# A recurrent layer's gates packed in three tiles of 128 rows, with the input split ahead of the gather

## The chip, the cores and the metric

One core of a Trainium2 chip runs the whole kernel. The metric is the device time of one execution in microseconds, the median of three runs. TensorE (PE) multiplies matrices, VectorE (DVE), ScalarE (ACT) and GpSimd (POOL) work on elements, and SyncE (SP) sends nearly all transfers; each engine takes its own instructions in order and waits for the others by semaphores.

## The reference, cut to what matters

The kernel computes two layers of a diffusion block on 512 latent and 256 context tokens. The change lies in the mixer of the second layer, a bidirectional gated linear recurrence with 16 heads of 88 channels (`D_RNN` = 1408):

```python
def rglru_coeffs(xb, w_a, b_a, w_x, b_x, lam):
    xh = xb.reshape(b, L, RG_HEADS, RG_DH)
    r = jax.nn.sigmoid(jnp.einsum('blhd,hde->blhe', xh, w_a).reshape(b, L, D_RNN) + b_a)
    gi = jax.nn.sigmoid(jnp.einsum('blhd,hde->blhe', xh, w_x).reshape(b, L, D_RNN) + b_x)
    log_a = (-RG_C * r) * jax.nn.softplus(-lam)
    a = jnp.exp(log_a)
    bx = jnp.sqrt(-jnp.expm1(2.0 * log_a)) * (gi * xb)
    return a, bx

# in bidir_rglru_mixer, for the latent tokens
z = h_lat @ w_in
gate = jax.nn.gelu(z[..., :D_RNN])
xl = depthwise_conv(z[..., D_RNN:], conv_w, conv_b, left=2)
af, bf = rglru_coeffs(xl, wa[0], ba[0], wx[0], bx[0], lam[0])
ab, bb = rglru_coeffs(xl, wa[1], ba[1], wx[1], bx[1], lam[1])
hf = linear_scan(af, bf, hf_c[:, -1], False)
hb = linear_scan(ab, bb, hb_c[:, 0], True)
y_lat = (gate * (hf + hb)) @ w_out
```

Each head thus has four gates: two (`wa`, `wx`) in each of two directions.

## The kernel before, in words

Channels lie on the 128 partitions, tokens along the free dimension, 768 of them (256 context, then 512 latent). Products in fp32 are made of three passes over two halves of each operand: a high half, which ACT or DVE casts to fp32r, and a low half, the difference. `mm3` (L260) sends the three passes, `split` (L256) makes the halves with `act.copy` and `dve.tensor_sub`, and `conv_w` with `halve` (L235, L247) does it for weights.

The recurrent mixer goes over 11 chunks of 128 channels, while the heads have 88 channels, so the two cut the 1408 channels differently; `rg_pieces` (L68) lists the 26 overlaps. For each chunk j:

- `xl_units(j)` (L1579) computes the input projection, 24 matmuls over each of two token ranges, and `xl_evac` (L1563) adds the convolution into a tile `xl` and sends the pieces of its rows by SP into one tile `hx` of 88 rows for each head (L1577).
- `head_units(h)` (L1635) splits `hx` into `xh` and `xlo`, and for each direction multiplies by the weights of two gates, 88 output rows each. ACT's `Tanh` (L1654) moves each gate from PSUM into a tile `tg`, two gates to a tile; the pieces go back by SP into tiles `th` that follow the chunks (L1660), one for each chunk and direction, four buffers in all.
- `rg_chunk(j)` (L1663) computes decay and input from `th` and `xl` (L1677 to L1692), scans (L1695 to L1699), multiplies with the gate and splits the result into `yh`, `yl`, written in place of `th` first (L1703 to L1707).
- `pg_units` (L1591) computes the product for the gate, and `w_out` (L1712) in three calls, after chunks 4, 7 and 10, the output product of three chunks with its addition to `x` in `residual` (L1081). The last two chunks' output product follows the stage.

`mix` (L1717) interleaves the heads of the next chunk with these products, so many units of filling for each unit of a head. The program's order is then a matter of a scheduler: the framework places the instructions of all engines by its own timeline, and each engine's order is fixed when the kernel is built. PSUM has two buffers of two banks (`mm`) for the heads and four of one bank (`sm`) for all else.

Of the kernel before, what the change touches and what calls it, by code (L numbers as in the profile page):

```python
# [9 lines left out]
F32 = mybir.dt.float32  # L10
F32R = mybir.dt.float32r
# [6 lines left out]
P = 128  # L18
# [29 lines left out]

PCOLS = {}
_n = 0  # L50
for _name, _w in (("b_ada0", 48), ("b_ada1", 48), ("mix_g0", 8), ("mix_g1", 8), ("ffn_g0", 8), ("ffn_g1", 8),
                  ("fin_g", 8), ("rcw", 44), ("rcb", 11), ("lam", 22),
                  ("c", 16), ("hcw", 36), ("hcb", 12), ("skip", 8), ("ln_g", 4)):
    PCOLS[_name] = (_n, _w)
    _n += _w
NPC = _n

NPL = PCOLS["c"][0]

PARTS = [[(i, min(i + 4, NPAIR)) for i in range(0, NPAIR, 4)], [(0, 20), (20, 22)]]  # L60

# [75 lines left out]
def layout(i):  # L137
    a = {}
    g = {k: np.asarray(v) for k, v in i.items()}
    xt = np.concatenate([g["ctx"][0], g["x"][0]], 0).T  # L140
    a["xs"] = np.ascontiguousarray(xt.reshape(KD, P, T))
    vec = lambda v: v.reshape(-1, P)
    rows = {
        "b_ada0": vec(g["b_ada"][0]), "b_ada1": vec(g["b_ada"][1]),
        "mix_g0": vec(g["norm_mix_g"][0]), "mix_g1": vec(g["norm_mix_g"][1]),
        "ffn_g0": vec(g["norm_ffn_g"][0]), "ffn_g1": vec(g["norm_ffn_g"][1]),
        "fin_g": vec(g["final_norm_g"]), "hcw": vec(g["hy_conv_w"][0]), "hcb": vec(g["hy_conv_b"][0]),
        "skip": vec(g["hy_skip"][0]), "ln_g": vec(g["sgu_ln_g"][0]), "rcw": vec(g["rg_conv_w"][0]),
        "rcb": vec(g["rg_conv_b"][0]),
        "lam": vec(g["rg_lam"][0]), "c": np.concatenate([vec(g["c"][0]), vec(g["c_ctx"])], 0),  # L150
    }
    a["prm"] = np.ascontiguousarray(np.concatenate([rows[k] for k in PCOLS], 0).T)
    a["w_ada"] = np.ascontiguousarray(g["w_ada"])
    a["wie"] = wtiles(g["w_in_even"][0])
    a["woe"] = wtiles(g["w_out_even"][0])
    a["wio"] = wtiles(g["w_in_odd"][0])
    a["woo"] = wtiles(g["w_out_odd"][0])
    for l in range(2):
        a[f"wfi{l}"] = wtiles(g["w_ffn_in"][l])
        a[f"wfo{l}"] = np.ascontiguousarray(wtiles(g["w_ffn_out"][l])[:, :, [k for p in PARTS[l] for k in paired(*p)]])  # L160
    rg = np.stack([g["rg_wa"][0], g["rg_wx"][0]], 1).transpose(3, 2, 0, 1, 4)
    a["rgw"] = np.ascontiguousarray(rg.reshape(RDH, NH // 2, 8 * RDH))
    hb = np.stack([g["rg_ba"][0], g["rg_bx"][0]]).reshape(64, RDH)
    a["hb"] = np.ascontiguousarray(hb.T)
    a["sw"] = np.ascontiguousarray(g["sgu_w"][0].transpose(2, 0, 1))
    a["sb"] = np.ascontiguousarray(g["sgu_b"][0].reshape(1, 512))
    a["f3w"] = np.ascontiguousarray(np.concatenate([g["hy_f3_w"][0], g["hy_f3_b"][0][None]], 0))
    c = constants()
    mlp = np.zeros((64, T + 131), np.float32)
    mlp[:33, 0:T] = c.pop("emb")  # L170
    mlp[:33, T:T + 64] = g["hy_f1_w"][0]
    mlp[:, T + 64:T + 128] = g["hy_f2_w"][0]
    mlp[:, T + 128:] = np.stack([g["hy_f1_b"][0], g["hy_f2_b"][0], g["hy_sin_freq"][0]], 1)
    a["mlp"] = mlp
    a.update(c)
    return a
# [3 lines left out]
def program(tc, A, out):  # L180
# [906 lines left out]
    def out_units(src, ks, xhi, xlo, off, mod_g, blks, nr=None, early=0, most=2):  # L1087

        n = len(ks)
        grp = min(most, 1024 // (n * P))  # L1090
        held, group = {}, []

        def weights(m):
            if W["rg"]:
                W["eng"] = dve, pool
            if grp == 1:
                return split_w(src(m), n * P)
            i = m % grp
            if i == 0:
                g = min(grp, KD - m)  # L1100
                with tc.high_priority(offset=W["pre"]):
                    raw = load_w(None, 0)
                    nc.sync.dma_start(raw[:, :g * n * P].rearrange("p (m c) -> p m c", m=g),
                                      src(slice(m, m + g)).rearrange("m p k c -> p m (k c)"))
                    group[:] = conv_w(raw, g * n * P)
            return [t[:, i * n * P:(i + 1) * n * P] for t in group]

        plan = [(m, b) for m in range(KD) for b in range(2)]
        h = max(KD - len(W["slots"]) * grp, 0)
        if nr:  # L1110
            plan = [(m, b) for m in range(h) for b in range(2)] + [(m, b) for b in range(2) for m in range(h, KD)]
        def unit(m, b, pa, part=slice(0, None)):
            t0, t1 = blks[b]
            wh, wl = held[m]
            for i, k in list(enumerate(ks))[part]:
                c = slice(k * P, (k + 1) * P)
                for pi, (w, x) in enumerate(((wh, xhi), (wh, xlo), (wl, xhi))):
                    pe.matmul(pa, w[:, c], x[k][:, t0 - off:t1 - off], start=(i == 0 and pi == 0),  # L1118
                              stop=(i == n - 1 and pi == 2))

        begun = {}
        if early:
            for m, b in plan[:4]:
                if b == 0:
                    held[m] = weights(m)
                begun[m, b] = smt()[:, 0:blks[b][1] - blks[b][0]]
                unit(m, b, begun[m, b], slice(0, early))
        for m, b in plan:
            t0, t1 = blks[b]
            if (m, b) in begun:  # L1130
                pa = begun[m, b]
                unit(m, b, pa, slice(early, None))
            else:
                if b == 0:
                    held[m] = weights(m)
                pa = smt()[:, 0:t1 - t0]
                unit(m, b, pa)
            residual(m, mod_g, pa, blks[b])
            if nr:
                nr.sumsq(m, xt[m], b, m > 4)  # L1140
                if b == 1 and m == (KD - 4 if grp > 1 and blks is SEGC else KD - 2 if grp > 1 else h):
                    nr.stats(0)
                if b == 1 and m == (KD - 1 if grp > 1 else h + 2):
                    nr.bc(0)
            yield
# [360 lines left out]
    sp = [spp.tile([P, 22], F32, name=f"sp{i}") for i in range(5)]  # L1506
    cq = c2.tile([P, 22], F32, name="cq")
    cq2 = c2.tile([P, 22], F32, name="cq2")
    hba = c2.tile([RDH, 64], F32, name="hba")
    nc.sync.dma_start(hba, A["hb"])  # L1510
    zz, nn, rr, ee, ss = sp
    dve.tensor_scalar_mul(zz, lam, -1.0)
# [50 lines left out]
    def xl_evac(j, ms):  # L1563
# [3 lines left out]
        for m, (c0, c1) in zip(ms, SEGC):  # L1567
            for kk, sh in ((0, -2), (1, -1), (3, 1)):
# [2 lines left out]
                dve.scalar_tensor_tensor(x[:, a:b], m[:, a + sh - c0:b + sh - c0], w, x[:, a:b],  # L1571
                                         op0=ALU.mult, op1=ALU.add)
        XL[j] = x
        for _, h, c0, h0, n in rg_pieces(j=j):
            if h not in HX:
                HX[h] = rg.tile([RDH, T], F32, tag="hx", bufs=2, name=nm("hx"))
            nc.sync.dma_start(HX[h][h0:h0 + n, :], x[c0:c0 + n, :])  # L1577

    def xl_units(j):  # L1579
        W["eng"] = act, dve  # L1580
# [54 lines left out]
    def head_units(h):  # L1635

        if h % 2 == 0:
            W["eng"] = act, dve
            HW[0] = split_w(A["rgw"][:, h // 2], 8 * RDH, rows=RDH)
        wh, wl = HW[0]  # L1640
        x = HX.pop(h)
        xh = wx.tile([P, 1024], F32R, tag="whi", bufs=1, name=nm("xh"))[0:RDH, 0:T]
        xl = wx.tile([P, 1024], F32R, tag="wlo", bufs=1, name=nm("xlo"))[0:RDH, 0:T]
        split(xh, xl, x)
        for d in range(2):
            t = rg.tile([RDH, 2, T], F32, tag="tg", bufs=2, name=nm("tg"))
            for mi in range(2):
                m = mmt()
                c = (h % 2 * 4 + d * 2 + mi) * RDH
                mm3([m[0:RDH, 0, 0:384], m[0:RDH, 1, 0:384]],  # L1650
                    [(wh[0:RDH, c:c + RDH], wl[0:RDH, c:c + RDH],
                      [xh[:, c0:c1] for c0, c1 in HALF], [xl[:, c0:c1] for c0, c1 in HALF])])
                b = 32 * mi + 16 * d + h
                act.activation(h3(t[:, mi, :]), m[0:RDH, :, 0:384], AF.Tanh, bias=hba[:, b:b + 1], scale=0.5)  # L1654
                if mi == 0:
                    yield
            for j, _, c0, h0, n in rg_pieces(h=h):
                if (j, d) not in TH:
                    TH[j, d] = rg.tile([P, 2, T], F32, tag="th", bufs=4, name=nm("th"))
                nc.sync.dma_start(TH[j, d][c0:c0 + n], t[h0:h0 + n])  # L1660
            yield

    def rg_chunk(j):  # L1663
# [46 lines left out]
    yh, yl = [], []  # L1710

    def w_out(k0, k1, nr=None):  # L1712
        return out_units(lambda m: A["woo"][m, :, k0:k1, :], range(k1 - k0), yh[k0:k1], yl[k0:k1], LC, g4, BLK1, nr)

    W["rg"] = True

    def mix(hs, fill, nf):  # L1717

        hu = [u for h in hs for u in [h] * 4]
        done = 0  # L1720
        gens = {h: head_units(h) for h in hs}
        for i, h in enumerate(hu):
# [20 lines left out]
    for j in range(NR):  # L1743
# [9 lines left out]
            n += 8  # L1753
        if j in (4, 7, 10):
            gens.append(w_out(j - 4, j - 1))
            n += 16
        if j == 4:
            dve.tensor_scalar_mul(g4, mod[1][1][:, :, 0:8], 0.25)
        gens.append(itertools.islice(last_mods, 1 if j > 4 else 2))
# [59 lines left out]
```

## Time and profile before

| | |
|---|---|
| median of three runs | 1833.41 us (1829.68 to 1834.64) |
| profiled execution, its own time | 1836.92 us |
| its span | 1835.1 us |
| PE / DVE / ACT / POOL busy in the span | 1689.9 / 1210.3 / 771.7 / 607.4 us |
| mean granted clock of PE, share of full | 0.955 |

The span runs from the first to the last instruction; the execution's own time is longer by what lies around it. A busy time is the sum over an engine's instructions. Matmuls are pipelined, so the distance between two starts says more of PE's pace than the duration of one, which holds a fill and a drain beside its columns.

### The profile page before, as it was taken

The numbers are of one execution on the slowest core, as the hardware profiler recorded it, in microseconds if no ns is written. First come the engines' busy times: TensorE is split into PE (matmuls) and PEld (weight loads), VectorE is DVE, ScalarE is ACT, GpSimd is POOL, SyncE is SP. The second block draws the span as 40 slices with busy tenths as digits, with TensorE's granted clock in tenths as the row PEclk, the third lists the DMA queues.
The fourth block names the chain that finished last, engine by engine and source line by source line (L and its number), as shares of the span: only waits on it lengthen the run. The fifth ranks groups of instructions, "written<-read, shape, count | busy, mean of one in ns | idle before, by whom it ended". The sixth has DMA issues, their size and how long they took to land. (4 is left out here: it accounts for less than half of the span.)

```text
span 1835.1 us, 23819 instructions
## 1 busy us (share of the span) xinstructions
PE 1689.9 (92%) x8968; PEld 1433.9 (78%) x8968; DVE 1210.3 (66%) x1883; ACT 771.7 (42%) x1224; POOL 607.4 (33%) x518
## 2 busy tenths in 40 slices
PE   5999999889889999999999898879996799999996
PEld 2576887679878989999999676667776778888885
DVE  7875766684887668777776848768889733333225
ACT  3643332222454555544454437655654432222212
POOL 4333132442466455655554213324343200000002
PEclk8999999899999999999999898889997899999998
DMA  8746232633115312121222145646553132222321
GB/s 289 233 146 235 87 113 72 244 113 127 58 39 179 116 58 81 58 81 58 81 69 69 58 134 168 191 125 177 157 170 108 48 126 92 92 92 83 89 81 46
DMA packets 78397, 213.00 MB, mean 116 GB/s; under 512 B 7610, under 2 KB 33354, under 8 KB 74186
## 3 DMA queue, kind: packets, MB, share of 16 engines
q1 hardware_dynamic: 75913, 204.67, 35.6%
q0 software_dynamic: 1792, 6.29, 0.9%
q8 instruction: 70, 1.15, 0.3%
q10 hardware_dynamic: 576, 0.52, 0.1%
q14 instruction: 46, 0.37, 0.1%
HBM read 178.30 MB, written 11.53 MB: 103 GB/s over the span
## 5 line engine op out<-in xcount | busy, mean ns | idle before, releaser
L250 DVE TENSOR_TENSOR wlo<-raw,whi 128x512 fp32r<-128x512 f32 (+2 forms) x300 | 307.4, 1039 | 311.0 <-ACT whi L249 305.0
L249 ACT CAST whi<-raw 128x512 fp32r<-128x512 f32 (+2 forms) x308 | 244.0, 810 | 421.3 <-PE mm L265 180.7
L397 POOL TENSOR_TENSOR ssum<-ssum,sq 128x256 f32<-128x256 f32 (+2 forms) x37 | 37.2, 1010 | 451.1 <-ACT sq L395 426.8
L250 POOL TENSOR_TENSOR wlo<-raw,whi 128x1024 fp32r<-128x1024 f32 (+1 forms) x31 | 75.0, 2421 | 143.7 <-DVE whi L249 73.4
L1118 PE MATMUL sm<-yh,whi 128*128 128x256 f32 (+1 forms) x304 | 98.4, 329 | 23.3 <-DVE x L1081 12.7
L1118 PE MATMUL sm<-yl,whi 128*128 128x256 f32 (+1 forms) x304 | 97.0, 319 | 0.0
L1118 PE MATMUL sm<-yh,wlo 128*128 128x256 f32 (+1 forms) x304 | 96.4, 318 | 0.0
L288 PE MATMUL sm<-hh,whi 128*128 128x512 f32 (+1 forms) x248 | 92.1, 372 | 1.2 <-DVE whi L249 0.7
L288 PE MATMUL sm<-hl,whi 128*128 128x512 f32 (+1 forms) x248 | 91.0, 367 | 0.0
L288 PE MATMUL sm<-hh,wlo 128*128 128x512 f32 (+1 forms) x248 | 90.4, 368 | 0.1
L1118 PEld LDWEIGHTS sm<-yh,whi 128*128 128x128 f32 x304 | 61.3, 203 | 29.8 <-DVE x L1081 15.0
L339 PE MATMUL sm<-ada,sct 128*32 128x512 f32 x384 | 74.5, 642 | 4.4 <-DMA ada<-in_w_ada_dram 2.8
L1654 ACT ACTIVATE tg<-mm,hba 88x768 f32<-88x768 f32 x64 | 55.8, 892 | 41.7 <-issue 22.8
L265 PE MATMUL mm<-hl,whi 128*128 128x512 f32 (+1 forms) x256 | 69.8, 347 | 0.0
L265 PE MATMUL mm<-hh,wlo 128*128 128x512 f32 (+1 forms) x256 | 69.3, 348 | 0.0
L265 PE MATMUL mm<-hh,whi 128*128 128x512 f32 (+1 forms) x256 | 68.5, 347 | 0.0
L1118 PEld LDWEIGHTS sm<-yl,whi 128*128 128x128 f32 x304 | 62.1, 204 | 0.0
L1118 PEld LDWEIGHTS sm<-yh,wlo 128*128 128x128 f32 x304 | 61.5, 203 | 0.0
L1332 POOL TENSOR_TENSOR u<-u,u 128x384 f32<-128x384 f32 x40 | 47.8, 1195 | 40.1 <-ACT u L1331 39.8
L288 PEld LDWEIGHTS sm<-hh,whi 128*128 128x128 f32 x248 | 48.6, 196 | 15.0 <-ACT whi L249 2.5
L1081 DVE SCALAR_TENSOR_TENSOR x<-sm,mod,x 128x128 f32<-128x128 f32 (+3 forms) x68 | 33.9, 501 | 35.2 <-PE sm L1494 18.1
L288 PEld LDWEIGHTS sm<-hh,wlo 128*128 128x128 f32 x248 | 48.3, 196 | 8.9 <-DVE wlo L250 0.9
(942 smaller groups left out, 5273.4 us busy)
## 6 DMA issues: line engine op xcount, KB each, us to landing
raw<-in_wfi_dram SPq DMA_DIRECT2D x88, 512.0 KB
ada<-in_w_ada_dram SPq DMA_DIRECT2D x32, 1024.0 KB
raw<-in_wfo_dram SPq DMA_DIRECT2D x38, 512.0 KB
ada<-in_w_ada_dram SPq DMA_DIRECT2D x24, 512.0 KB
raw<-in_wio_dram SPq DMA_DIRECT2D x22, 512.0 KB
raw<-in_wie_dram SPq DMA_DIRECT2D x20, 512.0 KB
th<-tg SPq DMA_DIRECT2D x12, 528.0 KB
kk<-kdx SPq DMA_DIRECT2D x16, 384.0 KB
```

The lines of the kernel that those rows point to most:

```text
L249: (h_.tensor_copy if h_ is not act else act.copy)(hi, src)
L250: l_.tensor_sub(lo, src, f(hi))
L265: pe.matmul(o, w, xx, start=(k == 0 and pi == 0), stop=(k == n - 1 and pi == 2))
L288: pe.matmul(self.outs[b], w[:, k * P:(k + 1) * P], x, start=(n == 0 and pi == 0), stop=(n == self.nk - 1 and pi == 2))
L339: pe.matmul(self.ps[32 * q:32 * q + 32, :], sct[:, 2 * k:2 * k + 32], self.w[k, q], start=(k == 0), stop=(k == KD - 1))
L397: (dve if late else pool).tensor_add(self.s[b], self.s[b], q)
L1081: dve.scalar_tensor_tensor(x, pa[:, s0 - t0:s1 - t0], mod_g[:, v, m:m + 1], x, op0=ALU.mult, op1=ALU.add)
L1118: pe.matmul(pa, w[:, c], x[k][:, t0 - off:t1 - off], start=(i == 0 and pi == 0), stop=(i == n - 1 and pi == 2))
L1332: pool.tensor_add(v, v, u)
L1654: act.activation(h3(t[:, mi, :]), m[0:RDH, :, 0:384], AF.Tanh, bias=hba[:, b:b + 1], scale=0.5)
```

## The change

Three parts, all in the recurrent mixer, and one of memory. (1) A head's four gates, 352 output rows, are cut into three tiles of 128, 128 and 96 rows instead of four of 88; a tile's rows belong to one, two or three gates, so the way back into `th` has more pieces, of 8 to 88 rows. (2) `xl_evac` splits the whole chunk into high and low halves, in one buffer each, and SP gathers both halves to the heads, into `hxh` and `hxl`. (3) `w_out` within the mixer works on all 512 latent tokens at once instead of twice 256. (4) Some parameter columns move from the tile that stays to the one that is freed early, and the bias table has another shape. Line numbers of the changed kernel are larger by 1 up to the split in `xl_evac`, by 4 or 5 behind it.

```diff
@@ xl_evac
         XL[j] = x
+        xs = [wx.tile([P, 1024], F32R, tag="w" + t, bufs=1, name=nm("x" + t))[:, 0:T] for t in ("hi", "lo")]
+        split(*xs, x)
         for _, h, c0, h0, n in rg_pieces(j=j):
             if h not in HX:
-                HX[h] = rg.tile([RDH, T], F32, tag="hx", bufs=2, name=nm("hx"))
-            nc.sync.dma_start(HX[h][h0:h0 + n, :], x[c0:c0 + n, :])
+                HX[h] = [rg.tile([RDH, T], F32R, tag="hx" + t, bufs=2, name=nm("hx" + t)) for t in "hl"]
+            for a, b in zip(HX[h], xs):
+                nc.sync.dma_start(f(a)[h0:h0 + n, :], f(b)[c0:c0 + n, :])
@@ head_units
-        x = HX.pop(h)
-        xh = wx.tile([P, 1024], F32R, tag="whi", bufs=1, name=nm("xh"))[0:RDH, 0:T]
-        xl = wx.tile([P, 1024], F32R, tag="wlo", bufs=1, name=nm("xlo"))[0:RDH, 0:T]
-        split(xh, xl, x)
-        for d in range(2):
-            t = rg.tile([RDH, 2, T], F32, tag="tg", bufs=2, name=nm("tg"))
-            for mi in range(2):
...
-            for j, _, c0, h0, n in rg_pieces(h=h):
-                if (j, d) not in TH:
-                    TH[j, d] = rg.tile([P, 2, T], F32, tag="th", bufs=4, name=nm("th"))
-                nc.sync.dma_start(TH[j, d][c0:c0 + n], t[h0:h0 + n])
+        xh, xl = HX.pop(h)
+        for i in range(3):
+            a, b = P * i, min(P * i + P, 4 * RDH)
+            t = rg.tile([P, T], F32, tag="tg", bufs=3, name=nm("tg"))
+            m = mmt()
+            c = h % 2 * 4 * RDH
+            mm3([m[0:b - a, 0, 0:384], m[0:b - a, 1, 0:384]],
+                [(wh[0:RDH, c + a:c + b], wl[0:RDH, c + a:c + b],
+                  [xh[:, c0:c1] for c0, c1 in HALF], [xl[:, c0:c1] for c0, c1 in HALF])])
+            act.activation(h3(t[0:b - a]), m[0:b - a, :, 0:384], AF.Tanh, bias=hba[0:b - a, 3 * h + i:3 * h + i + 1],
+                           scale=0.5)
+            for q in range(4):
+                d, mi = q // 2, q % 2
+                for j, _, c0, h0, n in rg_pieces(h=h):
+                    lo, hi = max(a, RDH * q + h0), min(b, RDH * q + h0 + n)
+                    if lo >= hi:
+                        continue
+                    if (j, d) not in TH:
+                        TH[j, d] = rg.tile([P, 2, T], F32, tag="th", bufs=4, name=nm("th"))
+                    o = c0 + lo - RDH * q - h0
+                    nc.sync.dma_start(TH[j, d][o:o + hi - lo, mi], t[lo - a:hi - a])
             yield
@@ w_out, out_units, mix
-        return out_units(lambda m: A["woo"][m, :, k0:k1, :], range(k1 - k0), yh[k0:k1], yl[k0:k1], LC, g4, BLK1, nr)
+        return out_units(lambda m: A["woo"][m, :, k0:k1, :], range(k1 - k0), yh[k0:k1], yl[k0:k1], LC, g4,
+                         BLK1 if nr else [(LC, T)], nr)
-        plan = [(m, b) for m in range(KD) for b in range(2)]
+        plan = [(m, b) for m in range(KD) for b in range(len(blks))]
-        hu = [u for h in hs for u in [h] * 4]
+        hu = [u for h in hs for u in [h] * 3]
@@ the chunk loop
             gens.append(w_out(j - 4, j - 1))
-            n += 16
+            n += 8
@@ parameters
-NPL = PCOLS["c"][0]
+NPL = PCOLS["b_ada0"][0]
...
-    hba = c2.tile([RDH, 64], F32, name="hba")
+    hba = c2.tile([P, 3 * NH], F32, name="hba")
```

The instructions also change places. On ACT, around the first activations of chunk 0 (`T_...<-th_...`, which wait for the gate rows of that chunk), before; `xh_10079` is the cast for head 2, `tg` are the gates of heads 1 and 2:

```order
L1654 ACTIVATE tg_9953<-mm_9954,hba 88x768
L1654 ACTIVATE tg_9953<-mm_9968,hba 88x768
L1677 ACTIVATE T_10048<-th_9865,cq 128x768
L1654 ACTIVATE tg_9988<-mm_9989,hba 88x768
L249 CAST whi_10254<-raw_10252 128x1024
L1678 ACT_TABLE_LOAD
L1678 ACTIVATE th_9865<-th_9865,cq_4340 128x768
L1654 ACTIVATE tg_9988<-mm_10010,hba 88x768
L257 CAST xh_10079<-hx_9816 88x768
```

And the same place now; `xhi_9939` is the cast of chunk 2, whose rows, with those of chunk 1, go to head 2:

```order
L1654 ACTIVATE tg_9907<-mm_9908,hba 96x768
L1654 ACTIVATE tg_9966<-mm_9967,hba 128x768
L250 CAST whi_10107<-raw_10105 128x1024
L258 CAST xhi_9939<-xl_9930 128x768
L1654 ACTIVATE tg_9988<-mm_9989,hba 128x768
L250 CAST whi_10264<-raw_10262 128x1024
L1654 ACTIVATE tg_10010<-mm_10011,hba 96x768
L1682 ACTIVATE T_10059<-th_9848,cq 128x768
```

The cast stood behind the first activations of chunk 0 and now stands ahead of them, and no cast stands between the gathered rows and the matmuls any more.

On SP, the gate rows of heads 0 and 1 (`th<-tg`) with what lies between them, before:

```order
L1660 DMA th_9865<-tg_9828 88x1536
L1660 DMA th_9914<-tg_9885 88x1536
L1577 DMA hx_9932<-xl_9922 88x768
L232 DMA raw_10486<-in_wio_dram 128x1024
L330 DMA ada_10198<-in_w_ada_dram 128x2048
L1660 DMA th_9865<-tg_9953 40x1536
L1660 DMA th_9977<-tg_9953 48x1536
```

And now, head 0 and the first tile of head 1:

```order
L1665 DMA th_9848<-tg_9839 88x768
L1665 DMA th_9848<-tg_9839 40x768
L1665 DMA th_9848<-tg_9877 48x768
L1665 DMA th_9887<-tg_9877 80x768
L233 DMA raw_10371<-in_rgw_dram 88x704
L1581 DMA hxl_9830<-xlo_9824 80x768
L1581 DMA hxh_9829<-xhi_9823 80x768
L1665 DMA th_9887<-tg_9907 8x768
L1665 DMA th_9887<-tg_9907 88x768
L1665 DMA th_9848<-tg_9966 40x768
L1665 DMA th_9976<-tg_9966 48x768
L1665 DMA th_9848<-tg_9966 40x768
```

Two transfers for head 0 have become six, each row half as long, and the inputs of the next head go as two transfers among them. Over the whole program the gate rows have 134 transfers instead of 52 and the head inputs 52 instead of 26; SP has 568 rows instead of 463, PE 288 head matmuls instead of 384 and 888 instead of 1104 matmuls of L1118.

## Rows read from the trace of the kernel before

**Rows 1.** The page, busy us of each engine, share of the span, instructions.
```profile
PE 1689.9 (92%) x8968; PEld 1433.9 (78%) x8968; DVE 1210.3 (66%) x1883; ACT 771.7 (42%) x1224; POOL 607.4 (33%) x518
```

**Rows 2.** Window of 1060 to 1420 us; the line of names says what the columns are.
```profile
core 0: us, PE busy (x) PEld busy (x) DVE busy (x) ACT busy (x) POOL busy (x), PEclk, DMA share, GB/s
...
1060.00:1420.00 360.00, 312.93 (x1675) 249.07 (x1676) 284.16 (x341) 200.70 (x237) 120.90 (x75) 0.90 0.55 156
```

**Rows 3.** Waits, 1060 to 1420 us: us in total, times, longest.
```profile
DVE th L1679 <- DMA th<-tg: 25.3, 10, 12.0
...
PE mm L265 <- ACT xh L257: 13.6, 5, 6.4
...
PE sm L1118 <- DVE x L1081: 12.7, 6, 8.3
...
PE mm L265 <- DVE xlo L258: 10.0, 5, 5.1
```

**Rows 4.** Timeline around 1099 to 1112 us: start, us, engine, instruction, idle before.
```profile
1099.40 0.96 DVE L1679 SCALAR_TENSOR_TENSOR th<-th,xl 128x768 f32<-128x768 f32 x1 [12.01 <-DMA th<-tg]
...
1105.97 1.58 PE L265 MATMUL mm<-xh,whi 88*88 88x384 f32 x4 [3.89 <-ACT xh L257]
...
1109.95 0.94 PE L265 MATMUL mm<-xlo,whi 88*88 88x384 f32 x2 [2.39 <-DVE xlo L258]
1110.69 0.84 PE L265 MATMUL mm<-xh,wlo 88*88 88x384 f32 x2
```

**Rows 5.** PE's timeline at full clock: 256 columns, pairs of 384, then 512.
```profile
1235.40 0.28 PE L1118 MATMUL sm<-yh,wlo 128*128 128x256 f32 x1
1235.52 0.28 PE L1118 MATMUL sm<-yh,whi 128*128 128x256 f32 x1
...
1236.22 0.51 PE L265 MATMUL mm<-xlo,whi 88*88 88x384 f32 x2
1236.57 0.51 PE L265 MATMUL mm<-xh,wlo 88*88 88x384 f32 x2
...
1290.03 0.40 PE L288 MATMUL sm<-hh,whi 128*128 128x512 f32 x1
1290.26 0.39 PE L288 MATMUL sm<-hl,whi 128*128 128x512 f32 x1
```

**Rows 6.** Groups by form: busy us, mean ns of one, idle before.
```profile
L1654 ACT ACTIVATE tg<-mm,hba 88x768 f32<-88x768 f32 x64 | 55.8, 892 | 41.7 <-issue 22.8 <-PE mm L265 12.6 <-DMA th<-tg 5.8
L1118 PEld LDWEIGHTS sm<-yl,whi 128*128 128x128 f32 x153 | 32.4, 212 | 0.0
L258 DVE TENSOR_TENSOR xlo<-hx,xh 88x768 fp32r<-88x768 f32 x16 | 25.1, 1567 | 7.0 <-ACT xh L257 7.0
...
L250 DVE TENSOR_TENSOR wlo<-raw,whi 128x768 fp32r<-128x768 f32 x20 | 21.9, 1094 | 0.1
L1081 DVE SCALAR_TENSOR_TENSOR x<-sm,g,x 128x256 f32<-128x256 f32 x64 | 29.3, 473 | 9.6 <-PE sm L1118 9.6
L1081 DVE SCALAR_TENSOR_TENSOR x<-sm,mod,x 128x512 f32<-128x512 f32 x16 | 12.0, 748 | 19.6 <-PE sm L1494 18.1 <-PE sm L1118 1.5
```

**Rows 7.** The chain of waits, seven gate transfers shown, shortest and longest: start, us.
```profile
1277.65 2.70 DMA th<-tg
...
1375.79 6.36 DMA th<-tg
```

**Rows 8.** SP's issues of gate rows and head inputs: ns min/median/max, first and last start.
```profile
L1660 SPq DMA_DIRECT2D th<-tg x52: 487/744/862, 1077.8 to 1384.5; - x52
...
L1577 SPq DMA_DIRECT2D hx<-xl x26: 542/766/1801, 1065.3 to 1332.1; - x26
```

**Rows 9.** SP's own waits, 1060 to 1420 us, the longest.
```profile
SPq L1660 <- ACT tg L1654: 51.9, 14, 7.8
```

**Rows 10.** Timeline at the end of chunk 3.
```profile
1212.04 0.69 DVE L258 TENSOR_TENSOR yl<-th,yh 128x512 fp32r<-128x512 f32 x1 [5.94 <-ACT yh L257]
...
1213.32 8.46 SPq L1660 DMA_DIRECT2D th<-tg  x4
```

More of the change, by code (lines that the diff above doesn't have):

```diff
@@ L50 @@
 _n = 0
-for _name, _w in (("b_ada0", 48), ("b_ada1", 48), ("mix_g0", 8), ("mix_g1", 8), ("ffn_g0", 8), ("ffn_g1", 8),
+for _name, _w in (("b_ada1", 48), ("mix_g1", 8), ("ffn_g0", 8), ("ffn_g1", 8),
                   ("fin_g", 8), ("rcw", 44), ("rcb", 11), ("lam", 22),
-                  ("c", 16), ("hcw", 36), ("hcb", 12), ("skip", 8), ("ln_g", 4)):
+                  ("b_ada0", 48), ("mix_g0", 8), ("c", 16), ("hcw", 36), ("hcb", 12), ("skip", 8), ("ln_g", 4)):
     PCOLS[_name] = (_n, _w)
@@ L162, in layout @@
     a["rgw"] = np.ascontiguousarray(rg.reshape(RDH, NH // 2, 8 * RDH))
-    hb = np.stack([g["rg_ba"][0], g["rg_bx"][0]]).reshape(64, RDH)
+    hb = np.stack([g["rg_ba"][0], g["rg_bx"][0]], 1).reshape(2, 2, NH, RDH).transpose(2, 0, 1, 3).reshape(NH, 4 * RDH)
+    hb = np.pad(hb, ((0, 0), (0, 3 * P - 4 * RDH))).reshape(NH * 3, P)
     a["hb"] = np.ascontiguousarray(hb.T)
@@ L1640, in head_units @@
         wh, wl = HW[0]
-        x = HX.pop(h)
-        xh = wx.tile([P, 1024], F32R, tag="whi", bufs=1, name=nm("xh"))[0:RDH, 0:T]
-        xl = wx.tile([P, 1024], F32R, tag="wlo", bufs=1, name=nm("xlo"))[0:RDH, 0:T]
-        split(xh, xl, x)
-        for d in range(2):
-            t = rg.tile([RDH, 2, T], F32, tag="tg", bufs=2, name=nm("tg"))
-            for mi in range(2):
[L1648 to L1656, printed above, removed]
-            for j, _, c0, h0, n in rg_pieces(h=h):
-                if (j, d) not in TH:
-                    TH[j, d] = rg.tile([P, 2, T], F32, tag="th", bufs=4, name=nm("th"))
-                nc.sync.dma_start(TH[j, d][c0:c0 + n], t[h0:h0 + n])
+        xh, xl = HX.pop(h)
[19 more added lines that the diff above has]
+                    nc.sync.dma_start(TH[j, d][o:o + hi - lo, mi], t[lo - a:hi - a])
             yield
```

## The prediction, made before the changed kernel had run

> **What bounds the kernel now.** I read the busy line of the page first: TensorE (PE) is busy 1689.9 us of a span of 1835.1 us [rows 1]. That invites the thought that every PE instruction saved is time saved, so the next view was the window of the stage that changes [rows 2]. The change touches one stage, from 1060 to 1420 us, the heads and chunks of the recurrent mixer. What stands before and after it works on the same data in nearly the same order. In that stage PE is busy 312.93 of 360 us at a mean granted clock of 0.90, VectorE (DVE) 284.16, ScalarE (ACT) 200.70. So no engine fills it: PE idles 47 us and runs part of the rest at the lower of its two clock levels (1.2 instead of 2.4 GHz).
>
> The waits of PE in the stage say why [rows 3]: 13.6 us on `xh` from ACT, 10.0 us on `xlo` from DVE, 12.7 us on the residual additions. The first two are the split of a head's gathered input into its two halves, done on ACT and DVE after the gather. One place in the timeline shows the mechanism [rows 4]: DVE idled 12.01 us until gate rows landed by DMA for chunk 0; the split of the next head stands behind that work in the orders of ACT and DVE, so PE idles 3.89 us for `xh`, then 2.39 us more for `xlo`. The pairs of matmuls behind the gap start 0.74 us apart; undisturbed they start 0.35 us apart [rows 5]. A gap costs twice: itself, and the lower clock behind it.
>
> **The change part by part.** I cost it against the profiled execution, 1836.92 us; the median of the three runs, 1833.41, is 3.5 us lower, and the difference found is taken off the median.
>
> *Head matmuls.* A head's four gates are 4 x 3 products x 2 halves of 384 columns, 12 pairs of matmuls; packed in three tiles they are 9 pairs. A pair takes 0.35 us from start to start at 88 rows [rows 5], and I take the same at 128 rows, as the time goes by columns (below): 3 x 0.35 x 16 heads = 16.8 us of PE work go. PE is not always what ends last here; the ends are 0 (all of it turns into idle time) and 16.8. I take half, 8.4 us, since 312.93 of 360 us are busy but the chunks are tied together by the loop named under the rivals.
>
> *Split ahead of the gather.* The split moves from each of 16 heads (88x768) to each of 11 chunks (128x768). DVE's subtraction takes 1.567 us now on average and 1.094 us at 128x768 elsewhere [rows 6]: 16 x 1.567 - 11 x 1.094 = 13.0 us of DVE. ACT loses five casts. The order on ACT, in the section on the change, shows what matters more: the cast that feeds head 2 now stands ahead of chunk 0's first activations, where it stood behind them. PE's 23.6 us on `xh` and `xlo` lose their cause. In its place PE waits for the gather itself, and for two transfers instead of one. Ends: 23.6 us gained, or 0 if the gather is as late. I take half, 11.8 us, because only the ACT and DVE hop goes, while the DMA, of some 2.7 to 6.4 us for transfers of this kind [rows 7], stays.
>
> *Gate activations.* 48 instead of 64 at 0.892 us [rows 6]: 14.3 us of ACT. ACT is busy 200.70 of 360 us [rows 2]; I count nothing, and if the cover fails this adds to the gain.
>
> *Output products over 512 tokens.* 432 matmuls of 256 columns become 216 of 512. Starts lie 0.12 us apart at 256 columns and 0.23 at 512 [rows 5]: two narrow ones cost 0.24, one wide one 0.23, so 216 x 0.01 = 2.2 us of PE, taken as nothing. A weight load takes 0.212 us [rows 6], longer than the 0.12 us between matmuls: loads run beside matmuls. With a load and its columns one behind the other, 0.12 = load + columns and 0.23 = load + twice the columns leave 0.01 us for a load. Were all of the 0.12 us the load's, dropping 216 would be worth 26 us at most. The Trainium skill ("TensorE: Matmul & The Clock Gate", Part 3) says that a weight load overlaps matmuls in flight only when its row group differs, which weights of all 128 rows never satisfy; by it these products would give those 26 us too. The trace does not agree: 0.01 us a load. The residual additions go from 48 at 0.473 us to 24 at 0.748 us [rows 6]: 22.7 - 18.0 = 4.7 us of DVE. PE waited 12.7 us for them, but 8.3 us of that is one wait [rows 3], where DVE was late with other work. Ends 0 and 12.7; I take 2.
>
> *Transfers.* Gate rows go out in 134 transfers instead of 52, head inputs in 52 instead of 26: 108 more on SP, at 0.744 and 0.766 us of issue [rows 8], 82 x 0.744 + 26 x 0.766 = 81 us of SP time. SP takes its work in order; it spends 52 x 0.744 + 26 x 0.766 = 59 us on these now. Most of the addition lies in SP's waiting time: its longest sums are waits for work that is not there yet, 51.9 us for gate activations alone [rows 9]. On the path is what stands between a head's last activation and the landing of its last piece. That grows by one or two issues per chunk, some 1.1 us x 11 = 12 us, and a last piece carries half the bytes, which takes some back: landings lie between 2.70 and 6.36 us [rows 7], the quicker ones for the smaller pieces. Ends: 0, and 41 us (below). I take 6 us lost.
>
> The reordered parameter columns are the same 289, loaded at the start in the same two transfers; 0, covered by the loads around them. The bias table is one small load long before it is used; 0.
>
> Sum: -8.4 - 11.8 - 2 + 6 = -16.2 us: 1820.7 against the profiled execution, **1817.2 us** against the median.
>
> **The rivals.**
> *No change (1833 us).* The chunks form a loop: the rows of chunk j+2 need a buffer that chunk j frees with its last instruction. In the trace DVE ends `yl` at 1212.73, SP sends gate rows from 1213.32 on [rows 10]. If this loop sets the pace, PE's 16.8 us become idle time, and what the split gives is eaten by the transfers: -11.8 + 12 = 0. For it: DVE's 79% in the stage and 25.3 us of DVE waiting for gate rows [rows 3]. Against it: DVE itself loses 13.0 + 4.7 us of work.
>
> *Slower (1852 us).* SP's queue. A tile now leaves in two to four transfers, three tile buffers go round, and ACT may not write a tile before the transfers of the one three back have landed; hi and lo of the next head stand in the same queue. If in each chunk three more gate issues and two more input issues stand ahead of what the chain waits for, that is (3 x 0.744 + 2 x 0.766) x 11 = 41 us against the 22.2 us gained: +19. It decides from the point where more than 2.0 us per chunk land on the path (22.2 / 11). For it: seven gate transfers lie on the piece of the chain shown for this stage [rows 7], and SP stands in order. Against: SP mostly waits now. The Trainium skill ("DMA: Bandwidth & Descriptors", Rules for kernel authors) asks for small transfers to be joined and calls those under 64 KB mostly overhead; the 8-row pieces, 24 KB, are such, and the change makes more of them.
>
> *Much faster (1795 us).* All 23.6 us of split waits and all 16.8 us go, with the clock steady, less 2 for transfers: -38.
>
> *The weight loads were on the path after all (1791 us).* -16.2 - 26 = -42. For it speaks only that a load is longer than the pitch; the 0.01 us above speaks against it.
>
> **How the numbers follow.** Chances: forecast (6 to 28 us gained) 0.50; much faster 0.12; weight loads 0.02; no change 0.15; slower 0.21. About 0.3% (5.5 us) is what a measurement can tell from no change: faster 0.64, same 0.15, slower 0.21. The range 1797 to 1842 takes in the forecast's own 1805 to 1827, the no-change case, and most of the slower one up to half its price, and leaves out about a fifth.
>
> **What would show it.** Right: PE's waits for `xh` and `xlo` are gone and no wait for the head inputs of like size has come; 288 head matmuls at the same pitch; the stage of 1060 to 1420 some 16 us shorter and what lies outside it unchanged; output products of 512 columns 0.23 us apart. Wrong: DVE's wait for gate rows grows beyond 25.3 us [rows 3], or ACT's wait to write a tile grows, or PE waits for head inputs: then SP's queue has taken it.

## The result, and the profile after

The changed kernel takes **1812.97 us** (median of 20 runs, 1808.21 to 1833.69) against 1834.53 us for the kernel before on the same chips (20 runs): a ratio of 0.9888, 95% interval 0.9873 to 0.9902, or 20.5 us less (18.0 to 23.3). The longest of the 20, 1833.69, ran at a granted clock of 0.903, the others at 0.955 to 0.967. The prediction was 1817.2 with a range of 1797 to 1842 and faster as the likeliest sign. The total came out; the runs below show that it is made up of other parts than the prediction's. The profiled execution took 1812.14 us with a span of 1810.2.

The page of the changed kernel, its busy line, answers to [rows 1]:

```profile
PE 1656.4 (92%) x8656; PEld 1408.9 (78%) x8656; DVE 1197.7 (66%) x1854; ACT 755.1 (42%) x1203; POOL 609.9 (34%) x518
```

PE loses 33.5 us of busy time and keeps its share. To see what the stage alone lost, take it from the first convolution activation into `xl` to the last cast into `yh`; in these bounds the windows of the kernel before and of the changed kernel read:

```profile
core 0: us, PE busy (x) PEld busy (x) DVE busy (x) ACT busy (x) POOL busy (x), PEclk, DMA share, GB/s
1059.70:1416.10 356.40, 309.85 (x1660) 246.00 (x1660) 282.25 (x337) 199.41 (x234) 120.82 (x74) 0.91 0.55 157
```

```profile
1054.30:1396.70 342.40, 287.83 (x1348) 223.75 (x1348) 271.05 (x308) 183.05 (x213) 121.24 (x74) 0.91 0.61 176
```

The stage is 14.0 us shorter. But it also **begins** 5.4 us sooner (1054.3 against 1059.7), and from its end to the end of the span are 413.5 us instead of 419.0. Some 11 us of the difference between these two executions lie where the change edits nothing.

The longest waits that bear on the prediction, 1054.3 to 1396.7 us of the changed kernel (us in total, times, longest), beside [rows 3]:

```profile
DVE th L1684 <- DMA th<-tg: 23.5, 10, 4.6
...
PE mm L266 <- ACT tg L1654: 14.7, 6, 6.0
...
PE sm L340 <- DMA ada<-in_w_ada_dram: 14.1, 5, 6.5
...
ACT tg L1654 <- DMA th<-tg: 11.1, 4, 4.6
...
PE sm L1119 <- DVE x L1082: 6.3, 4, 3.2
...
PE mm L266 <- DMA hxl<-xlo: 4.2, 3, 2.0
```

PE's 23.6 us on `xh` and `xlo` are gone, and only 4.2 us on gathered inputs came. Two waits are new: 14.7 us for ACT to empty a gate accumulator (0.6 us before), and 14.1 us for the loads of the modulation weights (`ada`), whose products, for the next layer's parameters, serve as filling work. DVE's wait for gate rows did not grow (25.3 to 23.5 us); ACT's wait to write a gate tile did, from 5.8 [rows 6] to 11.1 us.

The place of [rows 4] in the changed kernel's timeline:

```profile
1082.35 0.83 ACT L258 CAST xhi<-xl 128x768 fp32r<-128x768 f32 x1 [2.93 <-DMA hxh<-xhi]
...
1084.84 0.96 DVE L1684 SCALAR_TENSOR_TENSOR th<-th,xl 128x768 f32<-128x768 f32 x1 [0.67 <-DMA th<-tg]
...
1085.48 0.57 PE L266 MATMUL mm<-hxh,whi 88*128 88x384 f32 x2
```

Chunk 0's first instruction on DVE stands 30.5 us behind the start of the stage (1084.84 - 1054.3) with 0.67 us of waiting; before it was 39.7 us (1099.40 - 1059.7) with 12.01 us.

PE's pitches, from its timeline (compare [rows 5]), and SP's issues (compare [rows 8]):

```profile
1078.92 0.51 PE L266 MATMUL mm<-hxh,wlo 88*128 88x384 f32 x2
1079.27 0.51 PE L266 MATMUL mm<-hxh,whi 88*96 88x384 f32 x2
...
1225.65 0.39 PE L1119 MATMUL sm<-yl,whi 128*128 128x512 f32 x1
1225.87 0.40 PE L1119 MATMUL sm<-yh,wlo 128*128 128x512 f32 x1
1226.11 0.39 PE L1119 MATMUL sm<-yh,whi 128*128 128x512 f32 x1
```

```profile
L1665 SPq DMA_DIRECT2D th<-tg x134: 509/678/1547, 1070.6 to 1366.2; - x134
```

A pair of 128 output rows takes the same 0.35 us as one of 88, and 512 columns 0.23 us.

### The profile page after: what moved, and what is told of

The parts are those of the page before. It is cut to its first block, busy times and chain, and to the rows that moved or that the text cites. A ratio compares the mean times of both kernels' runs of the same rounds, so it can differ in the third digit from the quotient of the medians.

```text
span 1810.2 us, 23375 instructions
## 1 busy us (share of the span) xinstructions
PE 1656.4 (92%) x8656; PEld 1408.9 (78%) x8656; DVE 1197.7 (66%) x1854; ACT 755.1 (42%) x1203; POOL 609.9 (34%) x518
## 5 line engine op out<-in xcount | busy, mean ns | idle before, releaser
L251 POOL TENSOR_TENSOR wlo<-raw,whi 128x1024 fp32r<-128x1024 f32 (+1 forms) x31 | 75.9, 2450 | 139.7 <-DVE whi L250 30.8
L1119 PE MATMUL sm<-yh,whi 128*128 128x384 f32 (+2 forms) x232 | 84.3, 370 | 16.2 <-DVE x L1082 6.3
L289 PE MATMUL sm<-hh,wlo 128*128 128x256 f32 (+1 forms) x248 | 90.7, 369 | 0.0
L1119 PE MATMUL sm<-yh,wlo 128*128 128x384 f32 (+2 forms) x232 | 83.5, 361 | 2.7 <-POOL wlo L251 2.7
L1119 PE MATMUL sm<-yl,whi 128*128 128x384 f32 (+2 forms) x232 | 84.0, 362 | 0.0
L1119 PEld LDWEIGHTS sm<-yh,whi 128*128 128x128 f32 x232 | 46.2, 201 | 25.6 <-DVE x L1082 7.2
L289 PEld LDWEIGHTS sm<-hl,whi 128*128 128x128 f32 x248 | 49.3, 199 | 7.9 <-issue 1.9
L1654 ACT ACTIVATE tg<-mm,hba 128x768 f32<-128x768 f32 (+1 forms) x48 | 42.3, 896 | 27.3 <-PE mm L266 15.1
L1258 POOL TENSOR_TENSOR raw<-raw 128x512 f32<-128x512 f32 x20 | 27.9, 1398 | 72.7 <-DMA raw<-in_wfi_dram 55.2
```

The costliest lines, as they stand in the source:

```text
L251: l_.tensor_sub(lo, src, f(hi))
L289: pe.matmul(self.outs[b], w[:, k * P:(k + 1) * P], x, start=(n == 0 and pi == 0), stop=(n == self.nk - 1 and pi == 2))
L1258: pool.tensor_add(b1, b1, b2)
L1654: act.activation(h3(t[0:b - a]), m[0:b - a, :, 0:384], AF.Tanh, bias=hba[0:b - a, 3 * h + i:3 * h + i + 1], scale=0.5)
```

## The experiments

Theory A, formed from the two traces: the gain is made in the start-up of the stage and the rest of it goes at the pace of the loop over the gate-row buffers. Its rivals were the prediction's own sum (B), weight loads (C) and packing alone (D). Runs e1 to e4 share their runs of the kernel before, as do e5 to e8 and e9 to e12; across these groups the ratios are compared. Stage lengths are from each run's profile, in the bounds used above.

**e1: only the output products over 512 tokens**, in the kernel before:

```diff
-        return out_units(..., yh[k0:k1], yl[k0:k1], LC, g4, BLK1, nr)
+        return out_units(..., yh[k0:k1], yl[k0:k1], LC, g4, BLK1 if nr else [(LC, T)], nr)
...
-            n += 16
+            n += 8
```

> The kernel before with one part of the change: output products over 512 tokens. Theory A (the whole gain is made in the start-up of the stage, by the split standing ahead of the gather; later the chunks go at the pace of the loop over the buffers of the gate rows, so that work saved on PE turns into idle time): no change, 1834.5 within 3 us. Theory B (the sum of the prediction): 2 us less, 1832.5. Theory C (a weight load is on the path): 26 us less, 1808.

Measured: 1833.86 us, ratio 0.9993 (0.9981 to 1.0005); stage 357.2 us. No change. The 216 weight loads that went were worth 3.5 us at most, so C's 26 us are out.

**e2: only the packing**, with its 134 transfers; the split stays with the heads (`split(xh, xl, x)` back in `head_units`, whole `xl` rows gathered, output products of 256 columns). It has the new order of the parameter columns too.

> The kernel before with one part of the change: the gates packed in three tiles, with their 134 transfers; the split is still made per head behind the gather, the output products are of 256 columns. Theory A: no change or a small loss from the 82 transfers more, 1834 to 1838. Theory B: 8.4 us less for PE, 4.5 more for transfers, 1830.6. Theory D (packing is what gave the gain): 1815. The rival of the queue (3 x 0.744 x 11 = 24.6 us more, nothing for it): 1859.

Measured: 1818.73 us, 0.9909 (0.9894 to 0.9925); stage 349.1 us, and it begins at 1054.8 us. Far from A and from the queue's rival. PE's waits for the split in this run, with the split still at the heads:

```profile
PE mm L266 <- ACT xh L258: 5.2, 4, 1.9
...
PE mm L266 <- DVE xlo L259: 2.6, 2, 1.4
```

Packing alone takes them from 23.6 to 7.8 us.

**e3: split and packing**, output products of 256 columns:

```diff
-        return out_units(..., yl[k0:k1], LC, g4,
-                         BLK1 if nr else [(LC, T)], nr)
+        return out_units(..., yl[k0:k1], LC, g4, BLK1, nr)
...
-            n += 8
+            n += 16
```

> The changed kernel with output products of 256 columns again, so split and packing alone. Theory A: as the changed kernel, 1813 within 3 us. Theory B: 2 us more than the changed kernel, 1815. Theory C: 1839. With the run of packing alone it gives what the split is worth: 20 us by A, 13 by B (11.8 and its 1.5 of transfers), under 5 by D.

Measured: **1802.81 us**, 0.9843 (0.9820 to 0.9867); stage 334.2 us. Against e2 the split gives 12.1 us (0.0066 of 1834). PE's waits for the heads' inputs are no shorter for it: 6.0 us on `hxh` and 4.8 on `hxl`, where e2 had 7.8 on `xh` and `xlo`. What comes sooner is chunk 0's first instruction on DVE, 36.6 us behind the start of the stage in e2 and 30.8 in e3, with these lines in e2, then in e3:

```profile
1091.38 0.96 DVE L1684 SCALAR_TENSOR_TENSOR th<-th,xl 128x768 f32<-128x768 f32 x1 [10.18 <-DMA th<-tg]
```

```profile
1085.09 0.96 DVE L1684 SCALAR_TENSOR_TENSOR th<-th,xl 128x768 f32<-128x768 f32 x1 [0.80 <-DMA th<-tg]
```

Against e3 the changed kernel *loses* 8.3 us (0.0045) by its wide output products, which alone cost nothing in e1. Neither A nor B had that.

**e4: every gate transfer cut in two**, in the changed kernel:

```diff
-                    nc.sync.dma_start(TH[j, d][o:o + hi - lo, mi], t[lo - a:hi - a])
+                    for u0, u1 in HALF:
+                        nc.sync.dma_start(TH[j, d][o:o + hi - lo, mi, u0:u1], t[lo - a:hi - a, u0:u1])
```

> The changed kernel with each of its 134 gate transfers cut into two of 384 columns, 134 more issues of half the bytes: the price of an issue on SP. By the 6 us that the prediction took for 108 more: 7.4 us, 1820. By the rival of the queue (41 us for 5 issues more per chunk, here 12): 60 us or more, 1873. If SP's waiting time still holds them: 1813.

Measured: 1839.34 us, 1.0020 (1.0009 to 1.0031), 24.2 us above the changed kernel by the ratios (26.4 by the medians); stage 372.2 us. Its waits in the stage:

```profile
DVE th L1685 <- DMA th<-tg: 36.0, 11, 7.7
...
ACT tg L1654 <- DMA th<-tg: 32.0, 17, 4.7
...
PE mm L266 <- ACT tg L1654: 23.6, 9, 5.0
```

This is the chain that the prediction's slower rival described: ACT waits for a tile whose rows have not left (32.0 us, from 11.1), PE for ACT (23.6, from 14.7). SP's own waits for gate activations, its slack, are down to 10.8 us from 31.3. At 268 transfers SP's queue decides; a further transfer, of half the bytes, costs 24.2 / 134 = 0.18 us there.

**e5: only the new order of the parameter columns**, in the kernel before (the first hunk of the change, nothing else). PE's order is unchanged, row for row.

> The kernel before with one part of the change: the parameter columns in the new order (289 columns, two transfers). In the profiles of the three kernels that have it with packing, the stage begins 5 us sooner and what stands behind it is 6 us shorter than in the kernel before, with the same instructions there. Theory E (the columns do it): 11 us less, 1823 to 1826. The prediction (nothing): 1834.5 within 3 us; then the 11 us belong to packing or to chance.

Measured: 1825.07 us, 0.9955 (0.9938 to 0.9972): 8.3 us less. The stage begins at 1054.3 us, takes 355.8 us (356.4 before), and 412.6 us follow it (419.0 before). In a stretch behind the stage that PE fills without a gap, the window of the kernel before and of e5:

```profile
1500.00:1660.00 160.00, 160.00 (x687) 128.72 (x686) 52.39 (x56) 45.14 (x57) 0.00 (x0) 1.00 0.29 96
```

```profile
1500.00:1660.00 160.00, 160.00 (x701) 131.29 (x700) 54.29 (x58) 46.20 (x58) 0.00 (x0) 1.00 0.30 94
```

At a granted clock of 1.00 in both, PE has 701 matmuls in the 160 us instead of 687; by their starts they follow each other every 228.9 ns instead of 233.3. PE itself runs 2% quicker here.

**e9 and e10: the same without touching the parameters.** An unused tile behind them moves the weight tiles, and most others that follow, by 32 or by 64 bytes:

```diff
     prm = cst.tile([P, NPL], F32, name="prm")
+    pad = cst.tile([P, 8], F32, name="pad")
+    nc.vector.memset(pad, 0.0)
```

(16 columns instead of 8 in e10.)

> The kernel before with an unused tile of 8 columns (32 bytes) behind the parameters, so that the weight tiles and most others start 32 bytes further on; the parameter columns stand as before. In the new order of the columns these tiles start 224 bytes lower, that is 32 over a multiple of 64 instead of at one, and the products of 512 columns behind the stage follow each other every 229 ns instead of 233.5. Theory H (where the tiles start sets the pace of the products): as the run of the new order alone, 6 to 9 us less, 1825 to 1828. Theory I (the loads or the place of the parameters): no change, 1832 to 1835.

> The kernel before with an unused tile of 16 columns (64 bytes) in the same place. Theory H, if it is the place within 64 bytes that counts: no change, 1832 to 1835, 233.5 ns. If any shift does it: 1825 to 1828. Theory I: no change.

Measured: e9 1824.82 us, 0.9952 (0.9935 to 0.9969); e10 1833.97 us, 0.9997 (0.9983 to 1.0010). The same window in e9, then in e10:

```profile
1500.00:1660.00 160.00, 160.00 (x701) 131.28 (x700) 53.73 (x58) 46.10 (x57) 0.00 (x0) 1.00 0.29 95
```

```profile
1500.00:1660.00 160.00, 160.00 (x687) 128.51 (x687) 54.20 (x58) 46.75 (x59) 0.00 (x0) 1.00 0.28 92
```

32 bytes do it and 64 do not: the place of tiles within 64 bytes changes PE's pace in this stretch. By the memory map of the built programs all tiles of weight halves (`whi`, `wlo`) start at a multiple of 64 bytes in the kernel before, e1 and e10, and 32 bytes past one in e5, e9 and the changed kernel. The moving operands of this stretch (`b0h` to `b7l`) lie at the same addresses in the kernel before, e5, e9, e10 and the changed kernel, so it is not their place that makes the difference here. That the start of the weight tiles alone makes it is not shown either: output products of 512 columns, by the means of their starts, follow each other every 228.8 ns in e1, with weight tiles at multiples of 64 bytes, and every 233.2 ns in the changed kernel, with weight tiles 32 bytes past and `yh`, `yl` moved too.

**e6: wide output products in two steps**, in the changed kernel. A product of 512 columns hands over to the mixing with the heads once in the middle:

```diff
-                unit(m, b, pa)
+                if len(blks) == 1:
+                    unit(m, b, pa, slice(0, 2))
+                    yield
+                    unit(m, b, pa, slice(2, None))
+                else:
+                    unit(m, b, pa)
...
-            n += 8
+            n += 16
```

> The changed kernel, output products still 512 columns wide, but each product is handed to the mixing with the heads in two steps (16 steps per group instead of 8): the wide products cost 10 us beside split and packing. Theory F (the steps have become too long, so that the heads' tiles stand closer together and the loads of the modulation weights late): the 10 us come back, 1803 to 1806. Theory G (the width itself costs, by the residual of 512 columns or the accumulator): 1813 within 3 us.

Measured: **1801.55 us**, 0.9830 (0.9815 to 0.9845); stage 331.1 us. With the same 512 columns and the same instructions on PE it is 10.6 us (0.0058) below the changed kernel: the whole loss is gone. Against e3, with the same number of steps, the wide products are worth 2.4 us (0.0013), uncertain by some 5. What cost was the spacing: `mix` counts steps, not work, and with 8 long steps in place of 16 the scheduler sets every engine's order another way. Behind chunk 7 it shows best. The changed kernel's timeline there (`T<-T` begins the last part of chunks 7 and 8):

```profile
1297.28 1.48 ACT L1693 ACTIVATE T<-T 128x1536 f32<-128x1536 f32 x1
...
1301.99 1.68 ACT L1654 ACTIVATE tg<-mm,hba 96x768 f32<-96x768 f32 x2
...
1306.13 0.44 SPq L331 DMA_DIRECT2D ada<-in_w_ada_dram  x1
1306.67 0.88 SPq L233 DMA_DIRECT2D raw<-in_rgw_dram  x1
1307.64 1.94 SPq L1665 DMA_DIRECT2D th<-tg  x2
1310.11 0.77 SPq L1581 DMA_DIRECT2D hxh<-xhi  x1
1311.11 0.73 SPq L1581 DMA_DIRECT2D hxl<-xlo  x1
1311.89 8.11 SPq L1665 DMA_DIRECT2D th<-tg  x5
1316.04 1.03 ACT L1682 ACTIVATE T<-th,cq 128x768 f32<-128x768 f32 x1 [4.68 <-DMA th<-tg]
...
1338.80 1.49 ACT L1693 ACTIVATE T<-T 128x1536 f32<-128x1536 f32 x1 [10.76 <-DVE th L1686]
```

and that of e6:

```profile
1294.37 1.48 ACT L1698 ACTIVATE T<-T 128x1536 f32<-128x1536 f32 x1 [2.31 <-DVE th L1691]
...
1301.15 2.99 SPq L1670 DMA_DIRECT2D th<-tg  x4
...
1304.24 0.42 SPq L233 DMA_DIRECT2D raw<-in_rgw_dram  x1
1304.71 0.37 SPq L331 DMA_DIRECT2D ada<-in_w_ada_dram  x1
1306.37 1.03 ACT L1687 ACTIVATE T<-th,cq 128x768 f32<-128x768 f32 x1 [3.59 <-DMA th<-tg]
...
1327.34 1.49 ACT L1698 ACTIVATE T<-T 128x1536 f32<-128x1536 f32 x1 [2.05 <-DVE th L1691]
```

In the changed kernel two weight loads and the next head's inputs stand ahead of gate rows in SP's order, and chunk 8 starts its `T` 18.8 us behind chunk 7's `T<-T`; in e6 the gate rows go first and it is 12.0 us. From one `T<-T` to the next are 41.5 us and 33.0 us. By these rows the two loads hold SP for 1.5 us (1306.13 to 1307.64) and the two inputs for 1.8 (1310.11 to 1311.89), 3.3 of the 6.8 us between 18.8 and 12.0. So SP's order, which the prediction priced by its count of issues, mattered here by what stands ahead of what. This is one place, read in two traces. What makes the rest of the loss was not found, and SP's order was not tested by itself.

**e7: the two modulation products of a chunk apart**, in the changed kernel, to take away PE's 14.1 us on their loads:

```diff
-        gens.append(itertools.islice(last_mods, 1 if j > 4 else 2))
+        if j <= 4:
+            gens.insert(0, itertools.islice(last_mods, 1))
+        gens.append(itertools.islice(last_mods, 1))
```

> The changed kernel with the first of a chunk's two modulation products moved to the head of its filling work, so that the load of the second has the whole chunk to land. PE waits 14.1 us for these loads in the changed kernel, none in the kernel before. If that wait is on the path: 1801 to 1806. If it only stands in for another wait (gate tiles, chunks): 1813 within 3 us.

Measured: 1820.79 us, 0.9932 (0.9918 to 0.9946), 8.1 us *more* than the changed kernel by the ratios; stage 346.0 us. A miss. The wait that it aimed at fell, and the time rose:

```profile
PE mm L266 <- ACT tg L1654: 13.8, 6, 5.2
...
PE sm L340 <- DMA ada<-in_w_ada_dram: 5.7, 2, 4.7
```

So the 14.1 us were no price that could be had back by removing the wait; moving filling work ahead set the orders anew, and the time rose.

**e8: the head inputs on ACT's queue**, in e3 (`nc.scalar.dma_start` for the 52 transfers).

> Split and packing alone, its 52 transfers of head inputs issued by ACT instead of SP. If SP's order holds back gate rows or inputs: 3 to 8 us less than split and packing alone (1803), 1795 to 1800. If SP is not on the path: 1803 within 3 us. If ACT, which then pays each issue, is the narrow place: 52 x 0.7 = 36 us of ACT, up to 1820.

Measured: 1808.89 us, 0.9877 (0.9860 to 0.9894), 6 us more than e3; stage 341.2 us. Relieving SP gave nothing, and ACT pays: its own waits behind transfers grew from 12.2 to 18.0 us for a gate tile and from 6.5 to 12.7 us at the cast of `xhi`:

```profile
ACT tg L1654 <- DMA th<-tg: 18.0, 6, 5.9
...
ACT xhi L258 <- DMA hxh<-xhi: 12.7, 5, 4.9
```

**e11: gate rows one gate at a time, in the kernel before**, 104 transfers instead of 52:

```diff
-                nc.sync.dma_start(TH[j, d][c0:c0 + n], t[h0:h0 + n])
+                for mi in range(2):
+                    nc.sync.dma_start(TH[j, d][c0:c0 + n, mi], t[h0:h0 + n, mi])
```

> The kernel before with every transfer of gate rows cut into one per gate: 104 instead of 52, with half the bytes each. The price of a transfer where nothing else is changed. By the prediction (6 us for 108): 2.9 us more, 1836. By the run with 134 more in the changed kernel (26.4 us, 0.197 us each): 10 us more, 1843. If they hide in this kernel: 1833 within 3 us.

Measured: 1832.43 us, 0.9993 (0.9980 to 1.0006); stage 355.4 us. Nothing: 52 more transfers hide entirely, where e4's 134 more cost 0.18 us each. SP waits 79.4 us for gate activations here, against 10.8 in e4: a transfer cost nothing where SP had slack. PE's waits on the split in this run:

```profile
PE mm L265 <- ACT xh L257: 6.1, 4, 2.8
...
PE mm L265 <- DVE xlo L258: 1.4, 1, 1.4
```

They fell from 23.6 to 7.5 us, and the time stayed where it was; PE waits 9.8 us for ACT to empty a gate accumulator instead, 0.6 before. So the time did not hang on the waits that the prediction priced for the split.

**e12: both halves of a head's input in one tile and one transfer**, in e6, 26 transfers instead of 52:

```diff
+        xs = wx.tile([P, 2, 1024], F32R, tag="whl", bufs=1, name=nm("xhl"))[:, :, 0:T]
...
-            for a, b in zip(HX[h], xs):
-                nc.sync.dma_start(f(a)[h0:h0 + n, :], f(b)[c0:c0 + n, :])
+            nc.sync.dma_start(f(HX[h])[h0:h0 + n], f(xs)[c0:c0 + n])
```

> The changed kernel with its output products in two steps, as in the run before, and both halves of a head's input in one tile and one transfer: 26 transfers instead of 52. By 0.197 us a transfer: 5 us less than the 1801.6 of that run, 1796. If the first half now waits for the second and nothing is won: 1801 to 1806.

Measured: 1809.96 us, 0.9861 (0.9841 to 0.9881), 5.7 us more than e6 by the ratios, uncertain by 4.6; stage 338.1 us. A miss: fewer and larger transfers came out slower here. The waits that e6 had lost are back, on gate rows (DVE 11.7 us in e6) and on the modulation loads (3.7 us in e6):

```profile
DVE th L1693 <- DMA th<-tg: 24.3, 12, 3.8
PE sm L343 <- DMA ada<-in_w_ada_dram: 11.1, 4, 5.7
```

Three things changed at once, the joined wait, the weight halves that share this tile and are joined with it, and the scheduler's orders; they were not told apart.

## Why the prediction was right, and where it was not

The terms side by side, in us. The measured ones are differences of ratios, times 1834, each uncertain by some 3 to 5 us; the 6 us that the prediction took for 108 transfers are shared out by their number. The measured column adds up by construction, as each part is one run less another; in another order a part can differ, as the wide products do (e1). Each edit also sets the orders of all engines anew. In e7 and e12 that came with 6 to 8 us, and its share in the parts was not separated.

| part | predicted | measured | by |
|---|---|---|---|
| packing, with its 82 transfers | -8.4 + 4.6 = -3.8 | -8.4 | e2 less e5 |
| split ahead of the gather, with 26 transfers | -11.8 + 1.4 = -10.4 | -12.1 | e3 less e2 |
| output products over 512 tokens | -2 | +8.3 | changed kernel less e3 |
| parameter columns | 0 | -8.3 | e5 |
| sum | -16.2 | -20.5 | |

- *Head matmuls.* A pair of 128 rows takes 0.35 us, as predicted. That just half of the 16.8 us arrives holds if the transfers cost nothing; e2 cannot tell the two apart, and the half was a middle, not a reason.
- *Split.* Right in size, wrong in its working. The 11.8 us were half of PE's 23.6 us on `xh` and `xlo`. But packing alone took 15.8 us off these waits (e2), e11 took 16.1 us off them and gained nothing, and from e2 to e3 PE's waits for the heads' inputs rose from 7.8 to 10.8 us while 12.1 us were won. What the runs do bear out is the order that the prediction set beside this sum: with the casts ahead, chunk 0's first instruction on DVE comes 30.8 us behind the start of the stage in e3, where it came at 36.6 in e2 and 39.7 before. By the end of chunk 0's part on ACT (its `T<-T`) 7.7 of the 14.9 us by which e3's stage is shorter than e2's are won; where the rest is won was not found. Theory A overdid the start-up, and fell with e2: packing gives time of its own.
- *Transfers.* The +6 was a middle between "none" and "41". The runs show the ends, none in e11 and a queue that decides in e4; what the 108 cost in the changed kernel was not measured apart from the rest.
- *Output products.* This is the first term that failed. The prediction bounded it by 0 and 12.7 us gained, and did not ask whether it could lose. PE's and DVE's prices were right (e1 is no change, e6 is 2.4 us below e3, and DVE takes 736 ns for a residual of 512 columns where 748 was used). What it left out is that a step of filling work is also a unit of the mixing: 8 long steps instead of 16 set the orders another way, behind chunk 7 with gate rows behind weight loads on SP, and the stage lost 8.2 us (334.2 to 342.4), which e6 takes back. The sign holds only beside split and packing; e1's schedule had room for it.
- *Parameter columns.* The second: "0, covered by the loads around them" priced the loads and forgot that a tile of another size moves tiles behind it. The text said that what lies outside the stage would be unchanged; it lost about 11 us in the profiles, as it does in e5 (11.8 us) with nothing but the columns moved.
- *Rivals.* "Weight loads on the path" is refuted by e1, and with it what the Trainium skill ("TensorE: Matmul & The Clock Gate", Part 3) would give here, as the 0.01 us a load had said: the product with half its loads took the same time. "Slower by SP's queue" had the right chain, as e4 shows, with the wrong threshold; one of its signs, ACT's longer wait to write a gate tile, came in the changed kernel and did not decide there. "Much faster" (1795) came near in e6, at 1801.6, though 8.3 us of that are the tile starts. "No change" was wrong: 1833 lies outside the changed kernel's interval.
- *Joining transfers.* The Trainium skill ("DMA: Bandwidth & Descriptors", Rules for kernel authors) asks that small transfers be joined. Cutting the gate rows further cost 24.2 us in e4, in line with it; cutting them in e11 cost nothing, and in e12 joining came with 5.7 us more, which it does not lead one to expect.

So the sign held, and so did the chain of packed pairs and of the casts' order. That the total came this close is luck: two errors, -8.3 and +10.3 us, nearly cancel, and the split's size came out of waits that did not carry it.

Best of all versions run is e6, 1801.55 us; e3, at 1802.81, is not told apart from it.

## What to carry to other kernels

Price a step of filling work by what it does to the order as well as by its instructions: when a loop hands out steps by count, changing their size moves every queue, and a part that is free alone can cost time beside another (e1 against e3). Undo the parts one by one, in both directions, before crediting a sum; and when stretches that were not edited change their length, compare matmuls per microsecond there and shift the tiles by 32 bytes before looking for a cause in the edit. A wait's total is not what removing it returns: in e11 16.1 us of PE's waits went for nothing, and in e7, e8 and e12 three reliefs of named waits or queues came with 6 to 8 us more.

## What the runs showed of the hardware

The place of tiles within 64 bytes changes PE's pace in a stretch that it fills: matmuls of 512 fp32r columns start every 233.3 ns in the kernel before and 228.9 ns with the weight tiles and others moved by 32 bytes, at a granted clock of 1.00 in both, worth 8 to 9 us of the whole kernel (e5, e9). A shift of 64 bytes changed nothing (e10). The changed kernel shows 230.0 ns in the same window. The moving operands of this stretch did not move. Why was not found, and the start of the weight tiles alone does not order all products (228.8 ns in e1, 233.2 ns in the changed kernel, for the output products).

SP took 52 more transfers for nothing in the kernel before and lost 0.18 us for each of 134 more in the changed one, with issues of the same length (670 to 744 ns by the medians). SP's waits for gate activations were 79.4 us in the first case and 10.8 in the second; as kernel and row length differ too, that the slack makes the difference is not shown by itself.
